# First row tiles of six column groups multiplied by tokens that are not yet normed

## The chip, the cores and the metric

One core of a Trainium2 chip runs the whole program. The core has five engines that each work through their own instructions in order: TensorE (PE in the profile; PEld is its weight load), VectorE (DVE), ScalarE (ACT), GpSimd (POOL) and SyncE (SP), which here issues the loads of weights. The metric is the device time of one execution in microseconds. The kernel before took 1783.91 us (median of three runs, 1782.36 to 1784.23). The profiled execution took 1782.2 us; its span from the first to the last instruction is 1780.4 us.

## The reference, cut to what matters

One layer of a trunk with 128 context tokens and 256 latent tokens (384 in all), 2048 channels. Latent tokens get a position embedding. The part that matters here is the way into the first projection:

```python
def rmsnorm(x, g):
    y = x32 * lax.rsqrt(jnp.mean(x32 * x32, axis=-1, keepdims=True) + EPS)
    return y * g
...
sh1, sc1, g1, sh2, sc2, g2 = adaln(c, w_ada, b_ada)      # silu(c) @ w_ada + b_ada, two vectors c
h = rmsnorm(x, norm_mix) * (1.0 + sc1) + sh1
z = h @ w_in                                             # 2048 -> 5632 columns = 11 groups of 512
```

z is split among four token mixers (a gated recurrence of four heads, a spatial gating, a short convolution, a pooling), whose outputs go through w_out; a gated residual, a second adaLN norm, a gated MLP with a convolution (w_up, w_down), a gated residual and a last norm follow. adaLN vectors differ between context and latent tokens.

With A = norm_mix * (1 + sc1), B = sh1 and the norm's factor r (one number for each token), h = r * (A * x) + B, so h @ w = r * ((A * x) @ w) + B @ w.

## The kernel before, in words

**Layout.** Channels lie on the 128 partitions, tokens along the free dimension: x is 16 row tiles of 128 channels by 384 tokens, kept as x[0] to x[3] with four row tiles each. Every weight chunk is a load of 512 KB, 128 x 1024 f32 (`raw`). Products are made in three parts at a reduced format: ScalarE casts a chunk into `whi`, VectorE subtracts to get `wlo` (`Pipe.split`); tokens are split the same way into `hh` and `hl`; then `mm_a` (L517) or `mm_b` (L522) issue whi*hh, whi*hl and wlo*hh into one PSUM bank. `mm_b` makes the groups V and GBV with tokens on the partitions (three tiles of 512 columns); the other nine groups use `mm_a` (four tiles of 384 columns).

**Stages.** w_in is passed in three rounds over its row tiles: round 0 takes row tiles 0 and 1, round 1 takes 2 to 5, round 2 takes 6 to 15 (`ROUNDS`). In every round all 11 groups are passed; the sum of a round is evicted into SBUF as `z` (round 0: `ev_first`, a copy on ScalarE; later rounds: `ev_add`, an add on VectorE). In round 0 four groups come in pairs, one row tile at a time (`DUOS`: V with GBV, U with DX, function `win_duo`); the others (CC, CH, CB and heads H0 to H3) have one chunk of two row tiles each (`win_group`). The rounds are there because h of a row tile needs sc1 and sh1 of its 128 channels, which come out of w_ada, passed alongside: `ada_first(0)` and `ada_first(1)` (t0 and t1, four chunks each) give row tiles 0 and 1, `ada_start` gives two row tiles from eight chunks. When the last chunk of such a column is done, `columns` transposes and adds on VectorE, and `make_h` starts `h_make` for those row tiles: x times the norm's factor on VectorE, scale and shift on ScalarE, cast on ScalarE, difference on VectorE (`split_affine`).

**Order.** Everything is put in order when the program is written out. `Pipe` holds the list of chunks in TensorE's order. `Pipe.run` walks through it, keeps a planned time (`now`) and planned ends of VectorE, ScalarE and the load queue (`clock`), and between products lets threads (generators) issue their next instruction once their planned time is reached and the planned lag of VectorE and ScalarE is below 2.5 us. Casts of weights are threads with priority, started two chunks ahead. An engine works in the order in which instructions were issued, so a thread that is issued early and has to wait holds up what stands behind it. Loads go into two rings of five and four buffers and are issued by SP in chunk order, except those with a number `early`, which go first in that order. `merge_streams` mixes the adaLN chunks into the main chunks at a fixed rate. `need_h(n)` makes the threads issue what row tiles 0 to n-1 need.

**Start.** Ahead of `pipe.run` (L1192 to L1200): warm-up products, then for each of x[0] to x[3] the position add on VectorE and the squares on ScalarE, pair sums on VectorE, eight products with a matrix of ones that add the squares over channels and leave the sum on all partitions, square root on ScalarE and reciprocal on VectorE: `bc1`, the norm's factor. The loads of x[0] to x[3] go first on SP, then t0, d0 (V and GBV, row tile 0), t1's first chunk, d1 (U and DX, row tile 0), the rest of t1. No cast is let go ahead of h of row tile 0 (`hold`).

**PSUM.** Eight banks: four for the products' sums (`acc`), four for everything else (`misc`); an up group of the MLP takes three of the first and one of the second kind.

Of the kernel before, what the change touches and what calls it, by code (L numbers as in the profile page):

```python
# [14 lines left out]
P = 128  # L15
D = 2048
# [20 lines left out]

ROUNDS = ((0, 2), (2, 6), (6, 16))
# [6 lines left out]
WARM = (6, 8)  # L45
# [9 lines left out]
T_DMA = 1.46  # L55
TABLES = (AF.Silu, AF.Sigmoid, AF.Gelu_apprx_tanh, AF.Exp, AF.Sqrt)
# [35 lines left out]
class Pipe:  # L92
# [5 lines left out]
    def __init__(self, nc, pools, look_dma, look_split, backlog):  # L98
# [9 lines left out]
        self.clock = {"d": 0.0, "a": 0.0, "q": 12.0}  # L108
# [45 lines left out]
    hold = True  # L154
# [38 lines left out]
    def run(self):  # L193
        n = len(self.chunks)
        nxt, ahead, loaded = 0, 0, 0
        for c in sorted((c for c in self.chunks if "early" in c), key=lambda c: c["early"]):
            self.dma(c)
        for i in range(-1, n):

            while loaded < n:  # L200
                if "early" in self.chunks[loaded]:
                    loaded += 1
                    continue
# [30 lines left out]
def trunk(ctx, tc, a, o):  # L234
# [7 lines left out]
    psa = ctx.enter_context(tc.tile_pool(name="psa", bufs=4, space=PSUM))  # L242
    psm = ctx.enter_context(tc.tile_pool(name="psm", bufs=4, space=PSUM))
# [162 lines left out]
    n1 = {}  # L406
# [12 lines left out]

    def input_pairs(i):  # L420
        V.tensor_add(n1[i][:, 0:2], n1[i][:, 0:2], n1[i][:, 2:4])

    def input_sums(i):
        if i == 0:
            n1["ps"] = misc("ps_n1")
        for k in range(2):
            PE.matmul(n1["ps"][:, 0:T], ones, n1[i][:, k], start=i == 0 and k == 0, stop=i == 3 and k == 1)  # L427

    def input_norm():
        v1 = row_tile("v1")  # L430
        S.activation(v1, n1["ps"][:, 0:T], AF.Sqrt, bias=eps, scale=1.0 / D)
        V.reciprocal(bc1, v1)
# [110 lines left out]

    h_done, h_queue, h_workers = set(), [], []

    def h_worker():
        while h_queue:
            yield from h_make(h_queue.pop(0))
        h_workers.pop()

    def h_make(j):
# [3 lines left out]
        if j == 0:  # L555
            yield next(parts)
            pipe.hold = False
            pipe.finish(pipe.splits[0])
# [29 lines left out]
    def win_duo(i, k):  # L588
        def mm(c):
            need_h(k + 1)  # L590
            for n, grp in enumerate(DUOS[i]):
                n_acc, width = win_shape(grp)
                if k == 0:
                    z[grp] = slot(f"z{grp}", shape=(P, n_acc, width))
                for m in range(n_acc):
                    t = acc("acc0")
                    s = slice(512 * n, 512 * n + 512)
                    yield win_product(grp, t, m, k, c["hi"][:, s], c["lo"][:, s], True, True)
                    (ev_add if k else ev_first)(z[grp], m, t[:, 0:width])
        return dict(src=a["w_in_1"][i, k], mm=mm)  # L600

    def win_group(grp, rnd, evac):
# [4 lines left out]
        for k0 in range(k_lo, k_hi, 2):  # L607
            def pre(k0=k0):
                if rnd < 2 or grp == 0:
                    need_h(k0 + 2)  # L610
                if rnd == 2 and k0 == k_lo:
# [7 lines left out]
            def mm(c, k0=k0):  # L619
                if k0 == k_lo:  # L620
                    accs.extend(acc(f"acc{m}") for m in range(n_acc))
                    if rnd == 0:
                        z[grp] = slot(f"z{grp}", shape=(P, n_acc, width))
                hi = c["hi"].rearrange("p (k n) -> p k n", k=2)
                lo = c["lo"].rearrange("p (k n) -> p k n", k=2)
                for m in range(n_acc):
                    for kk in range(2):
                        yield win_product(grp, accs[m], m, k0 + kk, hi[:, kk], lo[:, kk], k0 + kk == k_lo, k0 + kk == k_hi - 1)
                    if k0 + 2 == k_hi:
# [267 lines left out]
    def rounds(rnd, evac):  # L897
# [3 lines left out]
        out.insert(1, win_duo(0, 1))  # L901
        out.insert(3, win_duo(1, 1))
        return out

    def make_h(js):
        h_queue.extend(js)
        for _ in range(min(2 - len(h_workers), len(js))):
# [413 lines left out]
```

## Time and profile before

| | |
|---|---|
| median of three runs | 1783.91 us (1782.36 to 1784.23) |
| the profiled execution | 1782.2 us |
| its span, first to last instruction | 1780.4 us |
| TensorE matmul busy | 1745.7 us, 98%, 11244 instructions |
| VectorE busy | 1111.8 us, 62%, 1911 instructions |
| ScalarE busy | 700.0 us, 39%, 1044 instructions |
| mean granted TensorE clock | 0.993 of full speed |
| read from HBM | 311.82 MB |

How to read it: matmuls are pipelined, so a busy TensorE is not one at its peak; a row of the timeline gives the start, the time to the end, the engine, the line of the code, the tiles (output, then inputs) and in brackets the idle time ahead of it and what ended it. Most instructions of VectorE and ScalarE stand at L88, the line of the helper that books them, so they are told apart by their tiles. A f32 matmul that is not in the reduced format leaves two records.

### The profile page before, as it was taken

What the parts mean: (1) busy time and instruction counts of PE and PEld (TensorE: products, weight loads), DVE (VectorE), ACT (ScalarE), POOL (GpSimd) and SP (SyncE); (2) the same over time, 40 slices, a digit from 0 to 9 for tenths busy, and PEclk for the clock granted to TensorE, in tenths of its full rate; (3) what the DMA queues carried; (4) which work ended last, traced back from release to release, by engine and by line L of the source; (5) the groups of instructions that cost most, each with busy time, mean ns of one, the idle gap of its engine ahead of it and who ended that gap; (6) DMA issues with size and microseconds to landing.
All of it is one profiled execution on the core that took longest, in us unless ns stands there. A gap on an engine that the chain in (4) does not pass through costs nothing.

```text
span 1780.4 us, 27719 instructions
## 1 busy us (share of the span) xinstructions
PE 1745.7 (98%) x11244; PEld 1681.1 (94%) x11244; DVE 1111.8 (62%) x1911; ACT 700.0 (39%) x1044; POOL 20.4 (1%) x35
## 2 busy tenths in 40 slices
PE   8999999999999999999999999999999999999996
PEld 6879889989999989999999999999999999999996
DVE  4585677888995577889884344455453445545454
ACT  5513333234753256344352223353332234434331
POOL 0000000000001000000000000000000000000000
PEclk9999999999999999999999999999999999999998
DMA  8878777576655764656654444434444444444431
GB/s 333 285 265 308 281 246 231 186 250 208 227 169 178 251 230 141 208 179 201 211 179 137 124 131 129 122 119 140 122 127 131 125 124 131 128 123 129 130 119 71
DMA packets 89664, 317.29 MB, mean 178 GB/s; under 512 B 9856, under 2 KB 14208, under 8 KB 89536
## 3 DMA queue, kind: packets, MB, share of 16 engines
q1 hardware_dynamic: 87520, 308.58, 53.5%
q0 software_dynamic: 1728, 6.55, 1.1%
q8 instruction: 88, 1.44, 0.3%
q10 hardware_dynamic: 288, 0.39, 0.1%
q14 instruction: 40, 0.33, 0.1%
HBM read 311.82 MB, written 3.67 MB: 177 GB/s over the span
## 4 chain that ended last, share of the span: by engine, by line
issue 63%; PE 30%; DVE 3%; DMA 2%; ACT 1%; SPq 0%; POOLq 0%; POOL 0%; DVEq 0%; ACTq 0%
PE acc L518 7%; PE acc L520 7%; PE acc L519 7%; PE ps_ada L463 3%; DMA raw<-in_w_in 1%; PE ps_sc L285 1%; PE acc L523 1%; PE acc L525 1%; PE acc L524 1%; DVE aacc L88 1%; DVE z L88 1%; DVE wlo L88 1%; DVE xr L88 0%; PE ps_n L427 0%; PE ps_o L285 0%
## 5 line engine op out<-in xcount | busy, mean ns | idle before, releaser
L88 DVE TENSOR_TENSOR wlo<-raw,whi 128x1024 fp32r<-128x1024 f32 x384 | 469.0, 1222 | 495.1 <-ACT whi L88 492.5
L88 ACT CAST whi<-raw 128x1024 fp32r<-128x1024 f32 x384 | 402.8, 1050 | 875.3 <-PE acc L519 625.0
L518 PE MATMUL acc<-h2h,whi 128*128 128x384 f32 x1408 | 471.6, 335 | 3.5 <-ACT h2h L88 3.4
L519 PE MATMUL acc<-h2l,whi 128*128 128x384 f32 x1408 | 471.1, 335 | 0.3 <-DVE h2l L88 0.3
L520 PE MATMUL acc<-h2h,wlo 128*128 128x384 f32 x1408 | 470.9, 334 | 0.0
L518 PEld LDWEIGHTS acc<-h2h,whi 128*128 128x128 f32 x1408 | 264.7, 188 | 5.1 <-ACT h2h L88 4.3
L519 PEld LDWEIGHTS acc<-h2l,whi 128*128 128x128 f32 x1408 | 264.8, 188 | 0.9 <-DVE h2l L88 0.9
L520 PEld LDWEIGHTS acc<-h2h,wlo 128*128 128x128 f32 x1408 | 264.7, 188 | 0.0
L520 PE MATMUL acc<-gh,wlo 128*128 128x384 f32 x704 | 235.1, 334 | 0.0
L518 PE MATMUL acc<-gh,whi 128*128 128x384 f32 x704 | 235.1, 334 | 0.0
L519 PE MATMUL acc<-gl,whi 128*128 128x384 f32 x704 | 235.1, 334 | 0.0
L518 PE MATMUL acc<-hh,whi 128*128 128x384 f32 x576 | 199.8, 347 | 4.2 <-DVE z L88 3.5
L520 PE MATMUL acc<-hh,wlo 128*128 128x384 f32 x576 | 193.3, 336 | 1.0 <-DVE wlo L88 1.0
L519 PE MATMUL acc<-hl,whi 128*128 128x384 f32 x576 | 192.8, 335 | 0.0
L88 DVE SCALAR_TENSOR_TENSOR aacc<-raw,svp,aacc 128x512 f32<-128x512 f32 x270 | 184.8, 745 | 0.0
L88 DVE SCALAR_TENSOR_TENSOR glu<-up,sm,glu 128x127 f32<-128x127 f32 (+1 forms) x352 | 135.3, 415 | 30.6 <-ACT glu L88 24.3
L518 PEld LDWEIGHTS acc<-gh,whi 128*128 128x128 f32 x704 | 132.1, 188 | 0.0
L519 PEld LDWEIGHTS acc<-gl,whi 128*128 128x128 f32 x704 | 132.1, 188 | 0.0
L520 PEld LDWEIGHTS acc<-gh,wlo 128*128 128x128 f32 x704 | 132.1, 188 | 0.0
L518 PEld LDWEIGHTS acc<-hh,whi 128*128 128x128 f32 x576 | 108.1, 188 | 16.7 <-issue 8.8
L520 PEld LDWEIGHTS acc<-hh,wlo 128*128 128x128 f32 x576 | 108.1, 188 | 1.6 <-DVE wlo L88 1.6
L519 PEld LDWEIGHTS acc<-hl,whi 128*128 128x128 f32 x576 | 108.2, 188 | 0.6
(154 smaller groups left out, 1540.6 us busy)
## 6 DMA issues: line engine op xcount, KB each, us to landing
raw<-in_w_up SPq DMA_DIRECT2D x176, 512.0 KB, 3.6
raw<-in_w_in SPq DMA_DIRECT2D x88, 512.0 KB, 5.2
raw<-in_w_down SPq DMA_DIRECT2D x88, 512.0 KB, 3.5
raw<-in_w_ada SPq DMA_DIRECT2D x64, 512.0 KB, 5.9
raw<-in_w_ada_dve SPq DMA_DIRECT2D x64, 512.0 KB, 4.5
raw<-in_w_ada_pe SPq DMA_DIRECT2D x64, 512.0 KB, 5.1
raw<-in_w_out SPq DMA_DIRECT2D x32, 512.0 KB, 4.5
x<-in_xT SPq DMA_DIRECT2D x4, 768.0 KB, 7.9
```

The source lines that it names most:

```text
L88: return f(*args, **kw)
L285: PE.matmul(out, *args, **kw)
L463: PE.matmul(ps[32 * s:32 * s + 32, 0:w], svp[:, 2 * k:2 * k + 32], raw[:, k - k0, s], start=k == 0, stop=k == KD - 1, tile_position=(0, 32 ...
L518: PE.matmul(out, wh, xh, start=first, stop=False)
L519: PE.matmul(out, wh, xl, start=False, stop=False)
L520: PE.matmul(out, wl, xh, start=False, stop=last)
L523: PE.matmul(out, xh, wh, start=first, stop=False)
L524: PE.matmul(out, xh, wl, start=False, stop=False)
L525: PE.matmul(out, xl, wh, start=False, stop=last)
```

## The change

The diff does these things:

- The groups U, DX, CC, CH, CB and H0 (`PLAIN`) take row tiles 0 and 1 as A * x in place of h: `plain_make` makes `uh` and `ul` from x, with two more columns that hold B for context and latent tokens; a product is then 386 columns wide, and the last two columns give B @ w. `fix` multiplies the evicted sums by `bc1` once it is there, and in round 1 `ev_shift` adds the two shift columns together with that round's sums.
- V, GBV and H1 to H3 still take h. Round 0's order becomes: U row tile 0, DX row tile 0, CC, CH, CB, H0, V/GBV row tile 0, V/GBV row tile 1, U/DX row tile 1, H1 to H3. U/DX row tile 0 (d0, d0b) are two chunks from one load, with t1 between them.
- The sums of squares become threads (`input_squares`, `input_norm`): the four sums over channels are added on VectorE, summed over partitions by products of one column, raised to the power -1/2 on POOL and broadcast by products, as at the second norm. The square root, the reciprocal and the 16 wide column-sum products of the start go away.
- Loads: x[0], positions, small tensors, t0, d0, t1, CC's chunk, then x[1] to x[3], then CH's chunk and the rest.
- For a group of round 0 in `PLAIN`, all products of the chunk's high part come first, then the low part tile by tile.
- `acc` has five banks and `misc` three; all four sums of an up group come from `acc`.
- Of the constants: fewer warm-up products (`WARM`), another rate of the adaLN chunks in round 0 (`AHEAD`), planned times of the loads of x (`X_THERE`, `T_X`), another first time of the load queue (`T_FIRST`).

```diff
+PLAIN = (W_U, W_DX, W_CC, W_CH, W_CB, W_H0)
...
-WARM = (6, 8)
+WARM = (6, 3)
+AHEAD = (0.0, 3.0, 1.0)
+X_THERE = (5.0, 21.0, 23.5, 26.0)
...
+T_X = 2.2
+T_FIRST = 3.0
...
-        self.clock = {"d": 0.0, "a": 0.0, "q": 12.0}
+        self.clock = {"d": 0.0, "a": 0.0, "q": T_FIRST}
...
-            if own and self.hold:
-                continue
...
+            if c["early"] in self.between:
+                self.between[c["early"]]()
+                self.clock["q"] += 3 * T_X
...
-    psa = ctx.enter_context(tc.tile_pool(name="psa", bufs=4, space=PSUM))
-    psm = ctx.enter_context(tc.tile_pool(name="psm", bufs=4, space=PSUM))
+    psa = ctx.enter_context(tc.tile_pool(name="psa", bufs=5, space=PSUM))
+    psm = ctx.enter_context(tc.tile_pool(name="psm", bufs=3, space=PSUM))
...
-    load_x(1, x[1], SY)
     S.dma_start(pos, a["pos_c"].rearrange("p k c -> p (k c)"))
-    load_x(2, x[2], SY)
-    load_x(3, x[3], SY)
+    pipe.between = {len_early: lambda: [load_x(i, x[i], SY) for i in range(1, 4)] for len_early in (10,)}
...
     def input_squares(i):
-        add_pos(x[i], i, pos, posr)
-        n1[i] = slot("sq0")
+
+        if i:
+            add_pos(x[i], i, pos, posr)
+            yield "d"
+        sq = slot("sq0")
         for k in range(0, 4, 2):
-            S.activation(n1[i][:, k:k + 2], x[i][:, k:k + 2], AF.Square)
+            S.activation(sq[:, k:k + 2], x[i][:, k:k + 2], AF.Square)
+            yield "a"
+        V.tensor_add(sq[:, 0:2], sq[:, 0:2], sq[:, 2:4])
+        yield
+        V.tensor_add(sqacc if i == 0 else sq[:, 0], sq[:, 0], sq[:, 1])
+        if i:
+            yield
+            V.tensor_add(sqacc, sqacc, sq[:, 0])
+        squared.append(i)
+
+    def input_norm():
...
+        ps = misc("ps_n1")
+        mean_square_rows(ps, sqacc)
+        yield 0.3
+        q = rstd_of(ps, NG, D, "n1")
+        yield 0.9
+        dgs = diags(q)
+        yield
+        bc = misc("ps_bc1")
+        broadcast_rows(bc, dgs)
+        yield 0.2
+        S.copy(bc1, bc[:, 0:T])
+        normed.append(1)
+        h_queue[:0] = [0, 1]
+        make_h((), 2)
+        for grp in PLAIN:
+            fixes[grp] = fix(grp)
+            pipe.spawn(fixes[grp])
...
+    def plain_make(j):
+        if not plain:
+            plain.extend(slot(n, F32R, (P, 2, T + 2)) for n in ("uh", "ul"))
+        uh, ul = plain[0][:, j], plain[1][:, j]
+        A, B, src = mods[:, 1, j], mods[:, 0, j], x[0][:, j]
+        for t0, t1, v in RANGES:
+            S.activation(uh[:, t0:t1], src[:, t0:t1], AF.Copy, scale=A[:, v:v + 1])
+        S.copy(uh[:, T:T + 2], B)
+        yield "a"
+        for t0, t1, v in RANGES:
+            V.scalar_tensor_tensor(out=ul[:, t0:t1], in0=src[:, t0:t1], scalar=A[:, v:v + 1], in1=uh[:, t0:t1].bitcast(F32), op0=ALU.mult, op1=ALU.subtract)
+        V.tensor_sub(ul[:, T:T + 2], B, uh[:, T:T + 2].bitcast(F32))
+        plain_done.add(j)
...
+    def fix(grp):
+
+        i = PLAIN.index(grp)
+        while grp not in summed or i and PLAIN[i - 1] not in fixed:
+            yield 0.3
+        for m in range(4):
+            zt = z[grp][:, m]
+            V.tensor_mul(zt, zt, bc1)
+            yield 1.2
+        fixed.add(grp)
+
+    def ev_shift(grp, zt, m, t):
+        for t0, t1, v in RANGES:
+            V.scalar_tensor_tensor(out=zt[:, m, t0:t1], in0=t[:, t0:t1], scalar=wb[grp][:, m, T + v:T + v + 1], in1=zt[:, m, t0:t1], op0=ALU.add, op1=ALU.add)
...
+    def plain_products(accs, hi, lo):
+        for m in range(4):
+            for kk in range(2):
+                for i in range(2):
+                    PE.matmul(accs[m][:, 0:T + 2], hi[:, kk, m * P:(m + 1) * P], plain[i][:, kk], start=kk == 0 and i == 0, stop=False)
+                    yield T_MM
...
-        out.insert(1, win_duo(0, 1))
-        out.insert(3, win_duo(1, 1))
+        out[len(PLAIN) - 2:len(PLAIN) - 2] = [win_duo(0, 0), win_duo(0, 1), win_duo(1, 1)]
...
-            t0, t1, d0, d1 = ada_first(0), ada_first(1), win_duo(0, 0), win_duo(1, 0)
-            for i, c in enumerate(t0 + [d0, t1[0], d1] + t1[1:]):
+            t0, t1, kept = ada_first(0), ada_first(1), {}
+            d0, d0b = win_duo(1, 0, 0, kept), win_duo(1, 0, 1, kept)
+            side = t0 + [d0] + t1 + [d0b]
+            for i, c in enumerate(t0 + [d0] + t1):
                 c["early"] = i
-            side = t0 + [d0] + t1 + [d1]
...
-            side = merge_streams(main, ada, count(ada) / (len(main) - 1.0))
+            if rnd == 1:
+                for i in range(2):
+                    main[i]["early"] = 9 + i
+            side = merge_streams(main, ada, count(ada) / (len(main) - AHEAD[rnd]))
...
-                    accs[1], accs[3] = acc("acc1"), misc("acc3")
+                    accs[1], accs[3] = acc("acc1"), acc("acc3")
...
-    pipe.chunks[4]["pre"] = lambda: (keep_warm(WARM[1]), need_h(1))
+    add_pos(x[0], 0, pos, posr)
+    for i in range(5):
+        stats.append(input_squares(i) if i < 4 else input_norm())
+        pipe.spawn(stats[i], X_THERE[i] if i < 4 else 0.0)
+    pipe.chunks[4]["pre"] = lambda: keep_warm(WARM[1])
```

## Rows read from the trace of the kernel before

**Rows 1.** TensorE's waits over the span: total, times, longest us.
```profile
PE acc L518 <- DVE z L88: 3.5, 4, 1.7
...
PE acc L518 <- ACT z L88: 0.7, 1, 0.7
PE ps_pool L285 <- DVE z L88: 0.6, 1, 0.6
```
**Rows 2.** Timeline of TensorE, 0 to 60 us: start, us, engine, line, operation, tiles.
```profile
4.69 5.12 PE L418 MATMUL ps_warm<-misc_c 128*128 128x256 f32 x12 [4.69 <-DMA misc_c<-in_misc]
12.90 7.26 PE L427 MATMUL ps_n<-sq,misc_c 128*128 128x384 f32 x16 [3.09 <-DVE sq L88]
20.10 1.99 PE L463 MATMUL ps_ada<-raw,svp 128*32 128x64 f32 x128
...
26.02 0.50 PE L523 MATMUL acc<-whi,hh 128*128 128x512 f32 x1 [0.28 <-ACT hh L88]
...
37.65 0.44 PE L518 MATMUL acc<-hh,whi 128*128 128x384 f32 x1 [0.73 <-ACT z L88]
...
41.74 0.34 PE L520 MATMUL acc<-hh,wlo 128*128 128x384 f32 x1
```
**Rows 3.** Timeline of VectorE, 0 to 60 us.
```profile
9.41 1.43 DVE L88 TENSOR_TENSOR x<-x,posr 128x256 f32<-128x256 f32 x4 [1.81 <-DMA x<-in_xT]
...
20.82 2.55 DVE L88 RECIPROCAL bc<-v 128x384 f32<-128x384 f32 x1 [2.49 <-ACT v L88]
23.29 0.19 DVE L88 STREAM_TRANSPOSE tr<-ps_ada 128x64 f32<-128x64 f32 x1
...
23.85 0.55 DVE L88 TENSOR_TENSOR ht<-x,bc 128x384 f32<-128x384 f32 x1
```
**Rows 4.** Timeline of ScalarE, 0 to 60 us.
```profile
10.30 3.02 ACT L88 ACTIVATE sq<-x 128x768 f32<-128x768 f32 x4
...
20.68 1.04 ACT L88 CAST whi<-raw 128x1024 fp32r<-128x1024 f32 x1
24.44 0.99 ACT L88 ACTIVATE ht<-ht,mods 128x128 f32<-128x128 f32 x2 [2.72 <-DVE ht L88]
...
33.23 0.48 ACT L88 COPY z<-acc 128x384 f32<-128x384 f32 x1 [1.49 <-PE acc L520]
```
**Rows 5.** Timeline of TensorE, 84 to 142 us.
```profile
85.19 0.39 PE L523 MATMUL acc<-whi,hh 128*128 128x512 f32 x1
...
107.30 0.45 PE L518 MATMUL acc<-hh,whi 128*128 128x384 f32 x1 [1.20 <-DVE z L88]
```
**Rows 6.** Windows: length, busy us of each engine (instructions), clock, DMA share, GB/s.
```profile
0.00:10.00 10.00, 5.12 (x12) 3.82 (x12) 2.13 (x7) 2.62 (x3) 0.53 (x8) 1.00 0.83 274
10.00:20.00 10.00, 7.09 (x16) 3.62 (x16) 7.18 (x15) 6.47 (x10) 0.00 (x0) 0.83 1.04 400
20.00:30.00 10.00, 9.72 (x162) 7.89 (x162) 5.21 (x8) 5.55 (x10) 0.00 (x0) 1.00 1.03 408
```
**Rows 7.** Windows of three stretches, same columns: PE, PEld, DVE, ACT, POOL.
```profile
62.00:85.00 23.00, 23.00 (x234) 21.21 (x233) 8.80 (x13) 15.53 (x30) 0.00 (x0) 1.00 0.87 304
85.00:131.00 46.00, 42.54 (x303) 36.82 (x305) 38.09 (x56) 12.38 (x16) 0.00 (x0) 1.00 0.70 250
131.00:200.00 69.00, 68.92 (x711) 63.52 (x700) 41.33 (x74) 24.95 (x37) 2.21 (x3) 1.00 0.86 307
```
**Rows 8.** VectorE's groups, 0 to 200 us: busy us, mean ns, idle before.
```profile
L88 DVE TENSOR_TENSOR wlo<-raw,whi 128x1024 fp32r<-128x1024 f32 x35 | 42.7, 1221 | 36.8 <-ACT whi L88 36.8
L88 DVE TENSOR_TENSOR z<-acc,z 128x384 f32<-128x384 f32 x43 | 22.2, 552 | 16.7 <-PE acc L520 16.5
...
L88 DVE TENSOR_TENSOR ht<-x,bc 128x384 f32<-128x384 f32 x14 | 7.3, 551 | 0.0
```
**Rows 9.** VectorE's groups, 500 to 660 us.
```profile
L88 DVE SCALAR_TENSOR_TENSOR xr<-acc,mods,xr 128x256 f32<-128x256 f32 x31 | 14.7, 475 | 0.0
L88 DVE SCALAR_TENSOR_TENSOR xr<-acc,mods,xr 128x128 f32<-128x128 f32 x31 | 10.7, 346 | 19.4 <-PE acc L520 19.4
```
**Rows 10.** Timeline of all engines at the last norm.
```profile
1765.78 1.65 PE L285 MATMUL ps_bc<-dg,misc_c 128*128 128x128 f32 x6 [1.50 <-DVE dg L88]
```

More of the change, by code (lines that the diff above doesn't have):

```diff
@@ L153 @@
     splits = []
-    hold = True
     def spawn(self, gen, delay=0.0):
@@ L200, in run @@
             while loaded < n:
-                if "early" in self.chunks[loaded]:
+                if "early" in self.chunks[loaded] or "src" not in self.chunks[loaded]:
                     loaded += 1
@@ L418, in keep_warm @@
             PE.matmul(ps[:, 0:2 * P], ident, misc_c, start=True, stop=True)
[L420 to L432, printed above, removed]
     def columns(ps, n, place):
@@ L542, in h_slots, with need_plain, plain_slot, ev_plain @@
         hl[i] = slot(f"{name}l{i}", F32R)
+    plain, plain_done, wb = [], set(), {}
+    def plain_make(j):
[11 more added lines that the diff above has]
+        plain_done.add(j)
+    def need_plain(n):
+        while not all(k in plain_done for k in range(n)):
+            for th in list(pipe.threads):
+                if th in pipe.threads and th[0] not in pipe.splits + stats:
+                    pipe.step(th)
+    def plain_slot(grp):
+        t = slot(f"z{grp}", shape=(P, 4, T + 2))
+        return t[:, :, 0:T], t
+    def ev_plain(grp, zt, m, t, add):
+        if add:
+            V.tensor_add(wb[grp][:, m], t[:, 0:T + 2], wb[grp][:, m])
+        else:
+            S.copy(wb[grp][:, m], t[:, 0:T + 2])
+        if m == 3 and (add or grp not in sum(DUOS, ())):
+            summed.add(grp)
+    def fix(grp):
+        i = PLAIN.index(grp)
+        while grp not in summed or i and PLAIN[i - 1] not in fixed:
+            yield 0.3
+        for m in range(4):
[6 more added lines that the diff above has]
+            V.scalar_tensor_tensor(out=zt[:, m, t0:t1], in0=t[:, t0:t1], scalar=wb[grp][:, m, T + v:T + v + 1], in1=zt[:, m, t0:t1], op0=ALU.add, op1=ALU.add)
     h_done, h_queue, h_workers = set(), [], []
@@ L547, in h_worker @@
         while h_queue:
+            while not normed:
+                yield 0.3
             yield from h_make(h_queue.pop(0))
@@ L586, in win_product, with plain_product, win_duo @@
         return 3 * T_MM
-    def win_duo(i, k):
-        def mm(c):
-            need_h(k + 1)
+    def plain_product(out, m, k, hi, lo, first, last):
+        w = slice(m * P, (m + 1) * P)
+        mm_a(out[:, 0:T + 2], hi[:, w], lo[:, w], plain[0][:, k], plain[1][:, k], first, last)
+        return 3 * T_MM
+    def plain_products(accs, hi, lo):
[4 more added lines that the diff above has]
+                    yield T_MM
+    def win_duo(i, k, part=None, kept=None):
+        def mm(c):
+            if part == 0:
+                kept.update(hi=c["hi"], lo=c["lo"])
+            if part == 1:
+                c = kept
+            need_plain(k + 1) if DUOS[i][0] in PLAIN else need_h(k + 1)
             for n, grp in enumerate(DUOS[i]):
+                if part not in (None, n):
+                    continue
                 n_acc, width = win_shape(grp)
-                if k == 0:
+                if k == 0 and grp not in PLAIN:
                     z[grp] = slot(f"z{grp}", shape=(P, n_acc, width))
@@ L597, in mm @@
                     s = slice(512 * n, 512 * n + 512)
+                    if grp in PLAIN and m == 0 and not k:
+                        z[grp], wb[grp] = plain_slot(grp)
+                    if grp in PLAIN:
+                        yield plain_product(t, m, k, c["hi"][:, s], c["lo"][:, s], True, True)
+                        ev_plain(grp, z[grp], m, t, k > 0)
+                        continue
                     yield win_product(grp, t, m, k, c["hi"][:, s], c["lo"][:, s], True, True)
                     (ev_add if k else ev_first)(z[grp], m, t[:, 0:width])
+        if part == 1:
+            return dict(mm=mm, split=False, there=0.0)
         return dict(src=a["w_in_1"][i, k], mm=mm)
@@ L913, in ada_first @@
         place = [(0, j, 1), (1, j, 1)]
-        return [dict(ada_pe(a["w_ada_0"][j, k4], (0, -j), 4 * k4, 4, place, lambda: make_h((j,))), spare=-1) for k4 in range(4)]
+        return [dict(ada_pe(a["w_ada_0"][j, k4], (0, -j), 4 * k4, 4, place, lambda: pipe.start(plain_make(j))), spare=-1) for k4 in range(4)]
     def ada_start(j2):
```

43 lines of the change are left out of this document (24 added, 19 removed).

## The prediction

> **What bounds the kernel now.** I read the busy table first: TensorE is busy for 1745.7 of 1780.4 us, so only what TensorE does not do counts. Next TensorE's waits over the span [rows 1]: in the stream of products little is left, 3.5 us for `z` evictions by VectorE (four waits) and 0.7 us for one by ScalarE. Then TensorE's timeline of the first 60 us [rows 2]. There lies the one large hole: the first product of a weight with tokens starts at 26.02. Ahead of it stand warm-up products (4.69), a wait of 3.09, the norm's column sums (12.90, 7.26 us) and one adaLN column (20.10, 1.99 us). The chain into 26.02 runs over two other engines: the reciprocal on VectorE at 20.82 (2.55 us), the adaLN column's transposition at 23.29, the multiplication by the norm at 23.85 [rows 3], then ScalarE's affine at 24.44 and the cast [rows 4]. After 26.02 TensorE is fed until round 1 begins at 85.19 [rows 5]. The windows say what is behind that: from 10 us to 30 us the loads run at 400 and 408 GB/s with a busy share above 1 [rows 6], so the order of the loads, not their sum, sets the first product; and from 85 us to 131 us VectorE is busy 38.09 of 46 us, which is where the 3.5 us are lost [rows 7].
>
> **The change part by part.**
>
> *Loads.* x1 to x3 (0.786 MB each) go behind t0, d0, t1 and CC's chunk (0.524 MB each). Bytes ahead: x0, posr, smalls, misc and pos 1.44 MB; t0 to 3.53; d0 4.06; t1 6.16; CC 6.68; x3 9.04; CH 9.56; the first adaLN pair 10.6. 2.74 MB have gone by 10.0 us, then 0.40 MB each us [rows 6]. x1, whose last byte is number 2.2 MB, is added to at 9.41 [rows 3], about 0.33 MB behind the stream. With that offset: t0 there at 12.8, d0 14.1, t1 19.4, CC 20.7, x1 22.6, x3 26.6, CH 27.9, the pair 30.5 us.
>
> *First product.* t0's last piece ends 0.5 us after 12.8 (1.99 for four [rows 2]), transposition and modulation 0.56 (23.29 to 23.85, [rows 3]), all before d0 is there. ScalarE has d0's cast ahead of the new `uh` in its order, as a cast whose chunk is due goes before the other threads: 14.1 + 1.05, then `uh` as two pieces of the affine's kind, 0.99, and a small copy 0.2: 16.4. VectorE: the low part of d0 1.22 [rows 8], then `ul`, two scalar-tensor-tensors that together take about 0.8 [rows 9], and a small one: 17.3. TensorE is dense from 17.3 where it was from 26.02: **-8.7 us**. The squares of x0 (3.02 of ScalarE for four, half of it here [rows 4]) run ahead of d0's landing and are hidden; without that cover 1.6 us.
> The pieces of `uh` have a pointer for the scale alone, the row has scale and bias. [...] The trace has no piece with one pointer, and I keep the row.
>
> *Waits on the way to round 1.* A group's 24 products take 4.2 us (37.65 to 41.74, [rows 2]). U ends at 19.4, t1's four pieces (1.99) at 21.4, DX at 23.5. But the order of the plan (by its own times DX's first tile is done at 19.4, CC's chunk there at 19.6, tile 1's column ready at 19.9) puts DX's first eviction (0.48 [rows 4]), CC's cast (1.05) and DX's second eviction ahead of `uh` of tile 1: 22.0, 22.5, 23.5, 24.0, so `uh` is there at 25.2, `ul` at 26.1; CC ends at 29.8, not 27.7: **+2.1**. CC's low part then ends on VectorE at 27.3, and the position add of x1 behind it (1.43 [rows 3]) at 28.7; ScalarE holds a square of x1 between CC's evictions, so CH's cast ends near 32.6, and TensorE, free at 31.0 after the pair, waits: **+1.7**. The squares of x2 and x3 push CB's cast: **+0.5**. The norm's two steps on TensorE wait for VectorE and POOL, **+0.5**, and work: six products by the identity and six small ones; six took 1.65 at half the clock [rows 10], so **+1.0** for both, between 0.8 and 2.7. 144 products get 2 more columns of 384 each: 0.1. Before, the same stretch had a wait of 0.7 that goes [rows 1]. Ends of the waits' sum: 0, if VectorE and ScalarE run the plan's order without blocking; 8, if each of x1 to x3 blocks a cast as x1 does.
> Sum to round 1: -8.7 + 2.1 + 1.7 + 0.5 + 0.5 + 1.0 + 0.1 - 0.7 = **-3.5**; it begins at 81.7.
>
> *Banks.* All four waits for VectorE in round 1 are first products of a group's tile that want a bank whose eviction stands behind a low part (107.30 after 1.20 [rows 5]). With five banks such a product finds the bank that was freed one tile (six products, 1.04 us) earlier; that takes away up to 3.5 [rows 1]. Three other banks in place of four: no wait of the span is for such a bank as it is, the nearest row is one of 0.6 us into `ps_pool` [rows 1]; I take nothing, the ends are 0 and 3 (a wait of that size once for each of four heads and the pool). acc3 moves to the same five banks: four per group of up, one spare, nothing.
>
> *Corrections.* `fix`: 24 multiplications of 0.55 [rows 8] are 13.2 us of VectorE; `ev_shift`: two scalar-tensor-tensors for one add, back to back 0.27 more, 24 times, 6.5. U is summed last, after the duo's second tile, so all `fix` come in the last three groups of round 0 and the first 20 us of round 1, about 1.7 us apart. 62 to 85 us has 14.2 us of VectorE free [rows 7] and hides half. The other 13 (7.2 us) and `ev_shift` of four groups (4.3) meet the stretch with 7.9 free. The ends: -3.5 (all hidden, all bank waits gone) and +11.5 (none of the idle time can be used). The nearest row is the one after it, 131 to 200 us, with 27.7 free of 69: a lag may drain there, as the casts run two chunks ahead. I take **-2.0** for banks and corrections together.
>
> Sum: -5.5 against the profiled execution's 1782.2 (span 1780.4): 1776.7. The median of the runs shown stands 1.7 above that execution: 1783.9 - 5.4 = **1778.5**.
>
> **The rivals.**
> *All hidden* (0.18): no cast is held up before CH and every bank wait goes: -8.7 + 1.1 - 0.7 - 3.5 = -11.8, **1772.1**. For it: the casts are asked for two chunks ahead. Against: from 16 us to 31 us ScalarE has two casts, twelve evictions, `uh` and four squares, 12.4 of 15 us.
> *The front gives it back* (0.22): each x tile blocks casts, the waits reach 8, and VectorE's extra work eats the banks' gain: about -1, **1783**. For it: VectorE and ScalarE work in order, and x1 to x3 now land among the first products. Against: each blocking ends with a landing, the last at 26.6.
> *VectorE takes over* (0.10), the other side: from 85 us to 131 us VectorE gets 11.5 us more and cannot use its idle time, which is waits for casts of weights not yet loaded. TensorE loses 11.5, less 3.5 of the front: +8, **1792**. It decides where VectorE's lag passes one bank's tile (1.04 us) and one cast ahead (a chunk, 4.2 us). Against: `fix` can come later, it is asked for only when its group is next.
> [...]
>
> **How the numbers follow.** The forecast has 0.45, with a range of its own of 1775.5 to 1781. 0.2% is 3.6 us, about what a measurement here tells from no change. Faster by more: nearly all of the forecast (0.43), all hidden (0.18), half of half clock and little of the second rival (0.04): 0.65. Slower: VectorE takes over, 0.10. The rest, 0.25, is within 0.2%. The range goes from 1771.5 to 1784.5: it holds the second rival and most of all hidden; beyond lie VectorE's case and the low end of all hidden.
>
> **What would show it.** First product with `uh` at 16 to 17 us, dense about 1 us later; round 1's first product of 512 columns near 82. Waits of TensorE for casts of CC and CH. No wait over 1 us for `z` between 85 and 131 us. VectorE over 8/10 busy from 66 to 105 us. Wrong: a first product later than 20 us, round 1 later than 84 us, or waits for `wlo` in round 1 of more than 4 us.

## The result, and the profile after

The changed kernel takes 1797.76 us (median of four runs, 1796.19 to 1799.13), the kernel before 1783.93 in the same session (four runs, 1782.36 to 1784.23): a ratio of 1.0078 [1.0066, 1.009], 13.8 us slower, where 1778.5 was forecast. The profiled execution of the changed kernel took 1799.1 us, its span is 1797.2.

**The front did what was forecast.** TensorE's timeline after the change (start, us, engine, line, operation, tiles, and in brackets the idle time ahead and what ended it):

```profile
15.59 0.45 PE L541 MATMUL acc<-uh,whi 128*128 128x386 f32 x1 [0.99 <-ACT uh L94]
16.80 0.44 PE L542 MATMUL acc<-ul,whi 128*128 128x386 f32 x1 [0.76 <-DVE ul L94]
17.07 0.40 PE L543 MATMUL acc<-uh,wlo 128*128 128x386 f32 x1
17.27 0.53 PE L541 MATMUL acc<-uh,whi 128*128 128x386 f32 x1
...
19.85 0.53 PE L543 MATMUL acc<-uh,wlo 128*128 128x386 f32 x1
20.30 2.12 PE L486 MATMUL ps_ada<-raw,svp 128*32 128x64 f32 x128
...
28.36 1.57 PE L736 MATMUL acc<-uh,wlo 128*128 128x386 f32 x8
30.35 0.64 PE L486 MATMUL ps_ada<-raw,svp 128*32 128x128 f32 x16 [0.42 <-DMA raw<-in_w_ada]
31.53 0.65 PE L486 MATMUL ps_ada<-raw,svp 128*32 128x128 f32 x16 [0.54 <-DMA raw<-in_w_ada]
...
80.86 0.39 PE L546 MATMUL acc<-whi,hh 128*128 128x512 f32 x1
```

The first product with `uh` starts at 15.59, the stream is dense from 16.80 where it was from 26.02 [rows 2], and round 1 begins at 80.86 where it began at 85.19 [rows 5]: 4.3 us earlier.

**The loss is in the long stages, in every product.** TensorE alone in two windows of the up and down stages, which the change doesn't touch (length, busy us and products, granted clock, DMA share, GB/s); first the kernel before, then after:

```profile
660.00:850.00 190.00, 189.84 (x1114) 1.00 0.57 177
1200.00:1600.00 400.00, 400.00 (x2309) 1.00 0.43 128
```

```profile
660.00:850.00 190.00, 190.00 (x1090) 0.98 0.56 175
1200.00:1600.00 400.00, 400.00 (x2281) 1.00 0.42 125
```

The same 400 us, TensorE busy throughout in both at full clock, hold 2309 products before and 2281 after. So one product starts 400 / 2309 = 173.2 ns after the other before, and 175.4 ns after (the step, in what follows; the expectations below have 173.3 and 175.5, taken from the starts of the products, as the count takes in those at the edges of the window). The busy share of the page says 98% for both kernels and shows nothing of this; nor do weight loads, whose mean is 188 ns in both. Where a product of the changed kernel stands against the same one of the kernel before, worked out from the two traces:

| product | before, us | after minus before, us |
|---|---|---|
| round 1, first | 85.2 | -4.3 |
| round 1, near 129 | 129 | -4.1 |
| last of the first projection | 464 | -1.9 |
| up stage, first | 656.3 | +2.3 |
| end of the span | 1780.4 | +16.8 |

From the first up product to the end 14.5 us are lost. 1.2 of them are gone by 666 us: TensorE waits 0.7 us longer for `h2l`, and the stage begins at half clock, which lasts longer than before (granted clock in 655 to 670 us 0.89 before, 0.77 after). The other 13.4 come with the products, 2.1 ns on each.

**TensorE's waits after**, over the span (total, times, longest), against [rows 1]:

```profile
PE acc L541 <- DVE z L94: 2.7, 1, 2.7
...
PE ps_sc L291 <- DVE z L94: 2.1, 2, 1.9
...
PE acc L543 <- DVE wlo L94: 1.2, 3, 0.6
...
PE ps_vt L937 <- DVE z L94: 0.8, 1, 0.8
...
PE acc L668 <- ACT whi L94: 0.2, 1, 0.2
```

The four waits for `z` (3.5 us) have become one of 2.7, and three waits of two kinds in the recurrence (`ps_sc`, `ps_vt`) are new. VectorE's busy time [rows 7] rose in 62 to 85 us from 8.80 to 17.91, in 85 to 131 us from 38.09 to 42.05:

```profile
62.00:85.00 23.00, 23.00 (x176) 21.33 (x177) 17.91 (x32) 13.00 (x23) 0.00 (x0) 1.00 0.70 248
85.00:131.00 46.00, 43.29 (x333) 38.40 (x333) 42.05 (x74) 8.40 (x8) 0.00 (x0) 0.96 0.75 261
```

### The profile page after: what moved, and what is told of

The parts are those of the page before. It is cut to its first block, busy times and chain, and to the rows that moved or that the text cites. A ratio compares the mean times of both kernels' runs of the same rounds, so it can differ in the third digit from the quotient of the medians.

```text
span 1797.2 us, 27779 instructions
## 1 busy us (share of the span) xinstructions
PE 1760.8 (98%) x11230; PEld 1698.3 (94%) x11230; DVE 1130.3 (63%) x1975; ACT 699.6 (39%) x1050; POOL 22.1 (1%) x36
## 4 chain that ended last, share of the span: by engine, by line
issue 64%; PE 27%; DVE 5%; DMA 2%; ACT 1%; POOLq 0%; POOL 0%; DVEq 0%; ACTq 0%
PE acc L541 6%; PE acc L543 6%; PE acc L542 6%; PE ps_ada L486 2%; DVE aacc L94 1%; DVE z L94 1%; DMA raw<-in_w_in 1%; PE acc L546 1%; PE acc L547 1%; PE acc L548 1%; DVE wlo L94 1%; PE ps_sc L291 1%; DVE hw L94 1%; ACT whi L94 1%; PE acc L668 0%
## 5 line engine op out<-in xcount | busy, mean ns | idle before, releaser
L541 PE MATMUL acc<-h2h,whi 128*128 128x384 f32 x1408 | 476.7, 339 | 2.9 <-ACT h2h L94 2.9
L542 PE MATMUL acc<-h2l,whi 128*128 128x384 f32 x1408 | 477.3, 339 | 1.0 <-DVE h2l L94 1.0
L543 PE MATMUL acc<-h2h,wlo 128*128 128x384 f32 x1408 | 475.8, 338 | 0.0
L541 PE MATMUL acc<-hh,whi 128*128 128x384 f32 x528 | 184.4, 349 | 2.7 <-DVE z L94 2.7
L543 PE MATMUL acc<-hh,wlo 128*128 128x384 f32 x528 | 178.7, 339 | 1.0 <-DVE wlo L94 1.0
L542 PE MATMUL acc<-hl,whi 128*128 128x384 f32 x528 | 178.5, 338 | 0.0
L541 PEld LDWEIGHTS acc<-hh,whi 128*128 128x128 f32 x528 | 99.6, 189 | 12.4 <-issue 9.5
L543 PEld LDWEIGHTS acc<-hh,wlo 128*128 128x128 f32 x528 | 99.6, 189 | 1.6 <-DVE wlo L94 1.6
L542 PEld LDWEIGHTS acc<-hl,whi 128*128 128x128 f32 x528 | 99.8, 189 | 0.6
```

What stands on the lines that cost most here:

```text
L541: PE.matmul(out, wh, xh, start=first, stop=False)
L542: PE.matmul(out, wh, xl, start=False, stop=False)
L543: PE.matmul(out, wl, xh, start=False, stop=last)
```

## The experiments

What could lengthen every product of stages that the change doesn't touch? Two things of the change reach that far: the banks (five and three), and the slots. All token tiles live in one pool of 20 slots, and a slot is as long as the largest tile. `z` of a `PLAIN` group has 4 x 386 words, so every slot grew from 6144 to 6176 bytes in each partition, and `hh`, `hl`, `h2h`, `h2l`, `gh`, `gl` lie elsewhere. The addresses below are those of the built kernels, as bytes within a partition; a residue is an address modulo 256. Before, all slots have residue 64 and all weight buffers too. The step is 400 us over the products in 1200 to 1600 us, in the one execution of each version that was traced.

**1. The kernel before with the changed kernel's slot length.**

```diff
-            return sp.tile(shape, dtype, tag="s", name=name)
+            return sp.tile([P, 1544], dtype, tag="s", name=name)[:, 0:1024]
```

> The kernel before with one thing of the change: every buffer of the 20-slot pool is 1544 numbers (6176 bytes) long where it was 1536 (6144); nothing is computed otherwise. Theory A (the longer slots make the token operands start at addresses that TensorE streams more slowly, 175.5 ns from product to product in the up and down stages of the changed kernel against 173.3 before): some 8800 products at +2.2 ns, +17 to +19 us, 1801 to 1803 us, and steps of 173 to 180 ns that differ by slot. Theory B (the five and three PSUM banks slow the products): no change, 1784 us, steps of 173.3. Theory C (the new start sets something later): no change, 1784 us.

Measured: 1789.35 us (before 1783.12), ratio 1.0034 [1.0021, 1.0046].

```profile
1200.00:1600.00 400.00, 400.00 (x2301) 1.00 0.42 126
```

The step is 173.8. Slot length alone makes the kernel before 6 us slower, a third of what was expected: the direction holds, the size not yet. (The tiles fall on other slots than in the changed kernel.)

**2. The changed kernel with slots of 6272 bytes**, a multiple of 128 (`[P, 1568]` in the same line).

> The changed kernel with slots of 1568 numbers (6272 bytes, a multiple of 128), nothing else. Theory A: steps go back to 173.3 ns, -17 to -19 us against the changed kernel, 1779 to 1781 us, so 3 to 5 us faster than before. Theory B: as the changed kernel, 1797 to 1798 us. Theory C: the same, 1797 to 1798 us.

Measured: 1796.68 us, ratio 1.0078 [1.0063, 1.0093]; 2285 products, step 175.1. Slots by turns at residue 64 and 192. Alignment to 128 bytes doesn't help here.

**3. The changed kernel with four and four banks; 4. the kernel before with five and three.**

```diff
-    psa = ctx.enter_context(tc.tile_pool(name="psa", bufs=5, space=PSUM))
-    psm = ctx.enter_context(tc.tile_pool(name="psm", bufs=3, space=PSUM))
+    psa = ctx.enter_context(tc.tile_pool(name="psa", bufs=4, space=PSUM))
+    psm = ctx.enter_context(tc.tile_pool(name="psm", bufs=4, space=PSUM))
...
-                    accs[1], accs[3] = acc("acc1"), acc("acc3")
+                    accs[1], accs[3] = acc("acc1"), misc("acc3")
```

(Experiment 4 is the same edit the other way round, on the kernel before.)

> The changed kernel with four and four PSUM banks and the fourth sum of an up group taken from the second kind, as before. Theory A: steps stay at about 175.5 ns; the waits of the recurrence near 483 us and 518 us (2.0 and 1.0 us) go, the waits for z in round 1 come back: 1794 to 1799 us. Theory B: steps go back to 173.3 ns, 1778 to 1783 us.

> The kernel before with five and three PSUM banks, the fourth sum of an up group from the first kind. Theory A: steps of 173.3 ns; of the 3.5 us of waits for z in round 1 most go, 1 to 3 us of waits come in the recurrence: 1781 to 1786 us. Theory B: steps of 175.5 ns, 1797 to 1800 us.

Measured: 3 takes 1794.21 us, ratio 1.0065 [1.005, 1.008], with 2281 products as in the changed kernel; 4 takes 1783.63, ratio 1.0002 [0.9993, 1.0012], with 2309. The banks have nothing to do with the step. What they do is seen in TensorE's waits. Experiment 4, over the span:

```profile
PE ps_sc L285 <- DVE z L88: 1.7, 2, 1.6
...
PE acc L518 <- DVE z L88: 1.1, 2, 0.8
...
PE ps_mod L500 <- DVE aacc L88: 0.8, 1, 0.8
PE ps_vt L825 <- DVE z L88: 0.8, 1, 0.8
```

Five banks cut the `z` waits from 3.5 to 1.1 us, and three small banks put 1.7 and 0.8 us into the recurrence and 0.8 into an adaLN column: a draw in time. In experiment 3 the recurrence has no such wait, and it is 3.5 us faster than the changed kernel; its granted clock also stays at 1.00 up to the end of the first projection, which the changed kernel's doesn't (0.96 in 85 to 131 us), so not all of that is shown to be the banks'.

**5. The changed kernel with slots of 6144 bytes again; 6. the same with four and four banks.** The two shift columns go into a small tile of their own, behind the slots.

```diff
-        t = slot(f"z{grp}", shape=(P, 4, T + 2))
-        return t[:, :, 0:T], t
+        return slot(f"z{grp}"), tmp.tile([P, 4, 2], F32, name=f"wb{grp}", tag=f"wb{grp}", bufs=1)
...
-            S.copy(wb[grp][:, m], t[:, 0:T + 2])
+            S.copy(zt[:, m], t[:, 0:T])
+            S.copy(wb[grp][:, m], t[:, T:T + 2])
```

> The changed kernel with its slots at 6144 bytes again: the two shift columns of each of the six groups go to a small tile of their own, so no slot is longer than 4 x 384 words; the eviction becomes two instructions (24 small copies on ScalarE and 8 small adds on VectorE more). Five and three banks stay. Theory A (the slower products come from where the slots lie): products of 384 columns start 173.3 ns apart again, 2.1 ns less than in the changed kernel, over 6336 products 13 us less: 1784 (1782 to 1787), about level with the kernel before, because the recurrence's waits with three banks eat what the front gained. Theory D (the step is longer because of something else that the change does, and the address is only a part of it, as the 0.5 to 1.5 ns of the first experiment suggest): the step stays at 174.5 or more and the time at 1791 or more. Theory F (the front gains nothing even with the slots where they were): 1784 to 1787 with round 1 not earlier than in the kernel before.

> The same with four and four banks and the fourth sum of an up group from the small ones, as in the kernel before: what is left of the change is the new start and the corrections. Theory A with the reading that three small banks cost 3.5 us in the recurrence: 1780.5 (1778 to 1783), 2 to 4 us faster than the kernel before; the step 173.3 ns. If the new start alone were worth the 8.7 us of the first product: 1775. Theory D: 1789 or more.

Measured: 1781.16 us (1780.0 to 1782.64), ratio 0.9986 [0.9977, 0.9995], and 1780.55, ratio 0.9986 [0.9978, 0.9995]. Experiment 5, the window and the waits of 470 to 520 us:

```profile
1200.00:1600.00 400.00, 400.00 (x2309) 1.00 0.43 128
```

```profile
PE ps_sc L291 <- DVE z L94: 1.7, 2, 1.5
PE ps_vt L938 <- DVE z L94: 0.8, 1, 0.8
```

The step is 173.2 again and 16.6 us are back, with all other parts of the change in place but for the evictions, now in two instructions. Together with experiments 1, 7 and 8, where nothing but addresses is changed, that makes the place of the slots the cause of the loss; theory D is out. The banks were not worth what the expectation of 6 said: in 6 the recurrence doesn't wait, but round 1's `z` waits are 3.6 us in four, and TensorE lost time earlier: it waited 1.85 us at 28 us for an adaLN load, and ran at half clock after that (window 30 to 40 us, granted clock 0.83):

```profile
30.00:40.00 10.00, 8.76 (x91) 0.83 1.03 408
```

**7 and 8. The kernel before with its slots moved, not lengthened.** All slots keep one residue.

```diff
+    gap = ctx.enter_context(tc.tile_pool(name="gap", bufs=1)).tile([P, 24], F32, name="gap")
     sp = ctx.enter_context(tc.tile_pool(name="sp", bufs=20))
```

(96 bytes; `[P, 32]` in experiment 8.)

> The kernel before with nothing changed but 96 unused bytes ahead of the slots: each slot is still 6144 bytes long, so all slots still have one residue to 256, 160 in place of 64. If it counts that slots differ in their residue (relation between the operands), the step stays 173.3 ns and the time 1783. If the residue itself counts (in the changed kernel and the first two experiments products that go from residue 160 to 160 took 178 ns), the step becomes 177 to 178 ns and the time 1783 + 6336 x 4.7 ns = 1813.

> The same with 128 unused bytes: residue 192 for all slots. Relation between operands: 173.3 ns, 1783. Residue itself: 175.8 ns (what 192 to 192 took in the second experiment), 1783 + 6336 x 2.5 ns = 1799.

Measured: 1810.42 us, ratio 1.0146 [1.0132, 1.016], and 1803.78, ratio 1.0112 [1.0098, 1.0126]. The windows of 7 and of 8:

```profile
1200.00:1600.00 400.00, 400.00 (x2266) 1.00 0.43 125
```

```profile
1200.00:1600.00 400.00, 400.00 (x2275) 1.00 0.42 125
```

96 unused bytes cost 27 us: 176.5 ns from product to product, 175.8 with 128 bytes. So it doesn't take unequal slots: where the slots lie is enough, as nothing else was changed here (the pools behind the slots move along, but hold no token operand of the up and down stages).

**9 to 12, 14, 15. The rest of the map.** The same line with `[P, 48]`, `[P, 8]`, `[P, 16]` and `[P, 64]` in experiment 6's version, with `[P, 40]` and `[P, 56]` in the kernel before.

> The version with four and four banks, slots of 6144 bytes, and 192 unused bytes ahead of the slots: residue 0 (to 256) for all slots, where it was 64. Theory R (the residue of the token operand's address sets the step, a value for each residue): before, 64 gave 173.3 ns, 160 gave 176.7, 192 gave 176.0. In the second experiment and the changed kernel, products that go from residue 0 to 0 took 173.3: step 173.3, time 1780.5 (1779 to 1783). Theory N (only 64 is good, as every other residue costs 2.5 to 3.5 ns): step 176, time 1797.

> The same with 32 unused bytes, residue 96. Theory R: 96 to 96 took 174.0 in the changed kernel: step 174.0, time 1785. Theory N: step 176, 1797.

> The same with 64 unused bytes, residue 128. Theory R: 128 to 128 took 173.9: step 173.9, time 1784. Theory N: step 176, 1797.

> The same with 256 unused bytes: residue 64 to 256 as in the kernel before, but 320 in place of 64 to 512. If 256 is the period, the step is 173.3 and the time 1780.5 (1779 to 1783). If the period is longer, the step differs by a nanosecond or more and the time by 6 us or more.

> The kernel before with 160 unused bytes ahead of its slots: residue 224 for all. The map so far: 0, 64, 96, 128 give 173.4 to 173.8 ns, 160 gives 176.7, 192 gives 176.0. If the slow residues are 160 to 224: step 176, time 1800. If only 160 and 192: step 173.4, time 1783.

> The same with 224 unused bytes: residue 32. It lies between two good ones (0 and 64): step 173.4 to 173.8, time 1783 to 1786; in the changed kernel products from 32 to 32 took 174.8, which would give 1792.

| experiment | residue of slots | products in 400 us | step, ns | time, us | ratio to before |
|---|---|---|---|---|---|
| 9 | 0 | 2309 | 173.2 | 1780.67 | 0.9983 [0.9973, 0.9992] |
| 15 | 32 | 2309 | 173.2 | 1784.26 | 1.0008 [0.9999, 1.0017] |
| 12 | 64 (320 to 512) | 2310 | 173.2 | 1780.35 | 0.9984 [0.9975, 0.9994] |
| 10 | 96 | 2310 | 173.2 | 1784.40 | 1.0003 [0.9994, 1.0013] |
| 11 | 128 | 2309 | 173.2 | 1780.74 | 0.9986 [0.9976, 0.9995] |
| 7 | 160 | 2266 | 176.5 | 1810.42 | 1.0146 [1.0132, 1.016] |
| 8 | 192 | 2275 | 175.8 | 1803.78 | 1.0112 [1.0098, 1.0126] |
| 14 | 224 | 2309 | 173.2 | 1783.83 | 1.0016 [0.9997, 1.0035] |

In this window six of eight residues are alike and two are slow; theory N is out, and so are the values that I had taken for 96, 128 and 32 from kernels with mixed slots. In experiment 10 some 4 us went elsewhere; part of it is that between 100 and 115 us its granted clock is 0.89. Experiment 12's version has the lowest time of all that were run, 1780.35 us, and beats the kernel before by 0.16%, as do 5, 6, 9 and 11 with nearly the same time.

The window isn't all of a trace. In experiment 9 two stretches of the up stage are slow although all its slots have the residue that the window calls good:

```profile
670.00:750.00 80.00, 80.00 (x460) 1.00 0.58 177
815.00:865.00 50.00, 50.00 (x285) 1.00 0.63 195
```

The kernel before has 464 and 291 products there. Taken from the starts of the products, experiment 9's step is 174.7 ns from 659 to 752 us, 176.7 from 810 to 872, and 173.3 between these and from there to the end. And of the ten executions of experiment 14, nine take 1782.8 to 1785.04 us and one 1802.01, about what experiment 8 takes; there is no trace of that one.

**13. Two good residues mixed.** The kernel before with slots of 6272 bytes that start at 128 and 0 by turns.

> The kernel before with slots of 6272 bytes that begin at residue 128 and 0 (to 256) by turns; each of the two alone left the step at 173.4 to 173.8 ns. Theory R1 (a product's step depends on its own operand's residue alone): step 173.6, time 1784.5. Theory R2 (a change of residue from one product to the next costs as well, as 192 to 64 at 179 ns in the second experiment suggests): step 174.5 or more, time 1790 or more.

Measured: 1787.94 us, ratio 1.0028 [1.0016, 1.0041]; 2304 products, step 173.6. A step near R1's, but a time between the two expectations: a mix of good places costs 0.4 ns a product, which is 2 to 3 of the 4.6 us; for the rest, 655 to 670 us is at a granted clock of 0.77 against 0.89. R2 holds in sign, with a small price, though residue 0 alone had slow stretches too (experiment 9).

**17 and 18. Slots or distance?** In all kernels so far the weight buffers had residue 64. In 17 the gap of 96 bytes stands ahead of the weight buffers, so weights and slots move alike; in 18 the slots get 160 bytes more.

```diff
+    gap = ctx.enter_context(tc.tile_pool(name="gap", bufs=1)).tile([P, 24], F32, name="gap")
     wp = ctx.enter_context(tc.tile_pool(name="wp", bufs=1))
```

> The kernel before with 96 unused bytes ahead of the weight buffers, which moves the weights and the slots alike: token operands at residue 160 as in the seventh experiment, weights at 160 too (there, and in all kernels so far, 64). Theory S (the token operand's own residue counts): step 176.7, time 1810. Theory W (the distance between weights and token operand counts; 96 and 128 bytes are the bad ones): the distance is 0 as in the kernel before, step 173.3, time 1783.

> The same with 160 more unused bytes between weights and slots: token operands at residue 64, weights at 160. Theory S: step 173.3, time 1783. Theory W: the distance is 160 (to 256), which the slots at 224 had too with 173.3: 1783 as well; so this run tells whether the weights' own residue costs: if it does, 176 and 1800.

Measured: 1782.45 us, ratio 1.0003 [0.9993, 1.0013], and 1785.66, ratio 1.0014 [1.0004, 1.0023]. The window of 17, and three windows of 18:

```profile
1200.00:1600.00 400.00, 400.00 (x2309) 1.00 0.43 128
```

```profile
670.00:750.00 80.00, 80.00 (x455) 1.00 0.53 162
820.00:870.00 50.00, 50.00 (x291) 1.00 0.65 208
1200.00:1600.00 400.00, 400.00 (x2309) 1.00 0.43 127
```

The kernel before in the first two of these:

```profile
670.00:750.00 80.00, 80.00 (x464) 1.00 0.55 168
820.00:870.00 50.00, 50.00 (x291) 1.00 0.61 189
```

Slots at residue 160, which cost 27 us in experiment 7, cost nothing when the weights stand at 160 too. So theory S is out: the token operand's own residue doesn't decide. The distance from the weights' address to the token operand's, modulo 256, sorts the window of all runs with equal slots: 0, 32, 64, 160, 192 and 224 bytes give 173.2 ns, 96 gives 176.5, 128 gives 175.8. That is as far as theory W is shown: both runs with the weights at 160 have distances that the map calls good (0 and 160), and no run puts 96 or 128 bytes between weights elsewhere than at 64 and their tokens.

Nor is the distance all of it. In experiment 18 the step itself changes within one execution: from the starts of the products it is 176.7 ns from 664 to 816 us, then come 16 small products of an adaLN column (`ps_mod`), and behind them it is 173.3 to the end, with the operands at the same residues. An earlier such group, at 758 us, had changed nothing. Against the kernel before, the same product stands 2.7 us later at 666 us and 5.0 later at 823 us, and no more than that at the end. So with the same addresses a stretch can run at either step. At 96 and 128 bytes every stretch of the up and down stages was slow, at 0, 32 and 64 none of the traced ones, and at 160 and 192 some were.

**16. CH's chunk ahead of the first adaLN pair**, in experiment 12's version.

```diff
+            n = 2 if rnd == 1 else 0
+            for c in main[:n]:
+                pipe.add(**c)
-            side = merge_streams(main, ada, count(ada) / (len(main) - AHEAD[rnd]))
+            side = merge_streams(main[n:], ada, count(ada) / (len(main) - n - AHEAD[rnd]))
```

> The twelfth experiment's version (1780.35; slots of 6144 bytes at residue 64, four and four banks), with CH's chunk right behind CC's in TensorE's order and the first adaLN pair behind it. In that version TensorE waits 0.62 us for the pair's load at 31 us and 0.54 us for CH's cast at 32 us, and in the sixth experiment 1.85 and 0.63 us there, with products at half clock until 36 us behind it. If these waits are what the front loses: 1778.5 (1777 to 1780). If CH's own load and cast come too late instead: 1780 to 1782.

Measured: 1780.81 us, ratio 0.9986 [0.9977, 0.9995]: no gain. TensorE now waits for the cast of CH's chunk instead, longer than for the pair before:

```profile
30.83 0.45 PE L670 MATMUL acc<-uh,whi 128*128 128x386 f32 x1 [2.59 <-ACT whi L94]
```

I read this as a stretch that the loads set (390 to 408 GB/s between 10 and 40 us in experiment 6), where each chunk that goes ahead puts off another; this was not tried further.

## Why the prediction was wrong, step by step

**The step that failed** is the one priced lowest: "144 products get 2 more columns of 384 each: 0.1". The two columns did cost little where they are computed: in the changed kernel DX's products of row tile 0, 386 columns wide, start 0.178 us apart (22.81 to 24.41 us), those of 384 columns 0.173 before. But they were stored in the slot of `z`, which lengthened all 20 slots, and with them the addresses of every token operand of the kernel changed. That term is not 0.1 but 16.6 us (experiment 5 against the changed kernel). I had read each edit by the instructions that it issues, and an allocation issues none. With that term taken out, the version comes to 1781.16 (five and three banks) and 1780.55 (four and four): inside the range, 2 to 2.7 us above the forecast.

**First product, -8.7: right.** First `uh` product 15.59 (16.4 forecast), dense from 16.80 (17.3). The two pieces of `uh` took 0.80 us together against 0.99 of the row [rows 4]: 0.1 us less for each. The row's pieces have scale and bias and those of `uh` the scale alone, but `uh` is also written in the reduced format, so what of it is the pointer's is not shown.

**Waits to round 1: right in sum, not in kind.** Round 1 begins at 80.86, forecast 81.7; of the 4.9 us given back on the way there, 1.3 are half clock, which the sum had as a rival and not as a term. The order that I read from the plan came out as written (DX's first eviction at 23.19, CC's cast at 23.57, `uh` of tile 1 at 24.52), and CC ends at 29.9 (29.8 forecast). But casts hold TensorE up by 0.2 us only; the waits at 30 us, 0.42 and 0.54, are for the adaLN pair's loads.

**Half clock: a rival that came true in part.** I had given it 0.05, at 1780.2 us, with 1.7 us for a stretch at half clock over U and t1. The changed kernel's trace doesn't show that 1.7, but 1.3 in U alone: from 17.27 us up to 20 us nine products take 0.32 us each in place of 0.18 (granted clock 0.54 in 17 to 20 us, 0.50 in 17.6 to 20.3), after TensorE had waited 0.99 and 0.76. t1's pieces behind them take 2.12 us against 1.99 [rows 2], and in 22 to 24 us the clock is 1.00 again. What makes it fall and come back is not shown: the two waits alone don't bring the fall, as experiment 6 has them too (1.00 and 0.76), and no fall. The changed kernel and experiment 6 in that window:

```profile
17.00:20.00 3.00, 3.00 (x11) 0.54 1.02 401
```

```profile
17.00:20.00 3.00, 3.00 (x95) 1.00 1.02 397
```

The same happened a second time, where I had not looked for it:

```profile
109.16 0.34 PE L543 MATMUL acc<-hh,wlo 128*128 128x384 f32 x1
112.21 0.41 PE L541 MATMUL acc<-hh,whi 128*128 128x384 f32 x1 [2.71 <-DVE z L94]
112.46 0.34 PE L542 MATMUL acc<-hl,whi 128*128 128x384 f32 x1
112.64 0.39 PE L543 MATMUL acc<-hh,wlo 128*128 128x384 f32 x1
112.82 0.53 PE L541 MATMUL acc<-hh,whi 128*128 128x384 f32 x1
...
115.70 0.53 PE L541 MATMUL acc<-hh,whi 128*128 128x384 f32 x1
116.02 0.42 PE L542 MATMUL acc<-hl,whi 128*128 128x384 f32 x1
```

**Banks and corrections, -2.0: too good.** "No wait over 1 us for `z`" was wrong. One wait of 2.71 us is left, and ten products at half clock behind it (0.50 in 113 to 116 us) cost 1.5 more: 4.2 in place of four waits of 3.5 in all that had left the clock alone (1.00 in 85 to 131 us before, 0.96 after). VectorE's order at that place:

```profile
107.07 1.22 DVE L94 TENSOR_TENSOR wlo<-raw,whi 128x1024 fp32r<-128x1024 f32 x1
108.21 0.55 DVE L94 TENSOR_TENSOR z<-z,bc 128x384 f32<-128x384 f32 x1
108.67 2.73 DVE L94 SCALAR_TENSOR_TENSOR aacc<-raw,svp,aacc 128x512 f32<-128x512 f32 x4
111.33 1.39 DVE L94 SCALAR_TENSOR_TENSOR z<-acc,z 128x128 f32<-128x128 f32 x4
```

A correction and four adaLN steps stand between a low part and the eviction; that is more than one more bank covers. In experiment 5 the lead over the kernel before is 3.1 us at round 1's start (82.05) and 3.5 at 200 us: banks and corrections together gave 0.4 there, not 2.0.

**Three small banks, taken as nothing with ends 0 and 3:** the upper end was the answer. 2.5 to 2.9 us of waits for `ps_sc` and `ps_vt` between 470 and 520 us stand in the changed kernel and in experiments 4 and 5, none in the kernel before, 3 and 6. The page couldn't show it, as no wait of the kernel before is for such a bank; the code could, as the recurrence holds several at once. Ahead of the longest of these waits in the changed kernel (1.88 us, up to 485 us) VectorE has a low part and adaLN steps of 2.73 us.

**VectorE takes over (the slower side):** its price was near the result, 1792, its mechanism not. `wlo` waits are 1.2 us after and 1.0 before.

**What stays open:** why 96 and 128 bytes are the bad distances (weight loads take 188 ns in the changed kernel as before), and what else sets the step of a stretch, as experiments 9 and 18 have both steps at the same addresses; how the step comes about where slots differ, since in the changed kernel about a fifth of the products has a bad distance, which by 3 ns each explains 0.6 of the 2.1 ns; and which of the half-clock stretches, in this place or that from one version to the next, account for the 1 to 3 us by which versions with the same step differ.

## What to carry to other kernels

An edit that makes one tile longer moves all tiles of its pool and of the pools behind it (here 32 bytes in each slot, which cost 16.6 us); work out the new addresses, and compare the number of products in an equal window of an untouched stage ahead of anything else. In a kernel with TensorE at 98%, the busy share doesn't show that each product has become 1% longer; the count in a window does (2309 before, 2281 after), and so does the mean of a group of products (335 ns before, 339 after for `h2h`). One window isn't enough: look at several stretches and at all executions. Several short waits can be cheaper than one long one, if TensorE's clock falls after the long one, as it did after 2.71 us here (0.50 in 113 to 116 us) and 2.35 in experiment 5 (0.32 us from product to product from 113.78 to 116.98 us, against 0.17 ahead); after 2.59 us in experiment 16 (up to 30.83 us) it stayed at 1.00.

## What the runs showed of the hardware that was not expected

In these runs the place of the token operands against the weights bears on the step of 384-column f32 products in the reduced format, with the same instructions at a granted clock of 1.00; what in the chip makes it so, no run shows. In the window of 1200 to 1600 us it is 173.2 ns at six of eight distances (multiples of 32 bytes modulo 256; in experiment 12, with slots 256 bytes further on, it is 173.2 as well), 176.5 at 96 bytes, 175.8 at 128. 96 unused bytes ahead of a pool made a kernel 27 us slower (1810.42 against 1783.39), and 96 ahead of both operands changed nothing (1782.45 against 1782.58). The distance alone doesn't set it: at 160 and at 192 bytes one execution had stretches at 176.7 ns and others at 173.3 (experiments 18 and 9). A mix of distances cost more than its parts, 2.1 ns in the changed kernel where a fifth of the products has a bad distance, 0.4 ns in experiment 13 where none has.
